# A two-layer encoder trunk on one Trainium2 core: P of two head groups turned by VectorE and DRAM, merged exits, new planner times

## The chip, the cores and the metric

The kernel runs on one core of a Trainium2 chip. The core has TensorE (matrix products; PE in the profile, with its weight loads as PEld), VectorE (DVE), ScalarE (ACT), GpSimd (POOL), SyncE (SP, which here only issues DMAs), and 16 DMA engines. TensorE writes into PSUM, eight banks of 512 f32 values in each of 128 partitions; the other engines read and write PSUM and the large on-chip memory SBUF. The metric is the device time of one execution in microseconds (us).

## The reference

Two layers work on x of 256 tokens by 1024 channels, all in f32:

```
x = x + 0.5 * swiglu(rmsnorm(x))                 # 1024 -> 2 x 2816 -> 1024
h = rmsnorm(x);  q_s, k_s, v_s, q_m = h @ w_in   # 1024 -> 768 + 768 + 768 + 256
layer 0: p = softmax(rmsnorm(q) k^T * scale + rel_bias), masked by chunks of 64 tokens   (12 heads of 64)
layer 1: p = softmax(q1 k1^T) - lam * softmax(q2 k2^T), with rotary and the block-causal mask (6 double heads)
o_s = p @ v;   o_m = 4-head attention into 256 memory tokens
x = x + concat(o_s, o_m) @ w_out
x = x + 0.5 * swiglu(rmsnorm(x))
```

swiglu(h) = (silu(h @ w_gate) * (h @ w_up)) @ w_down. The weights come from DRAM once, some 190 MB read in one execution.

## The kernel before

**Products.** Every f32 weight block is split into hi, rounded to the type fp32r, and lo = w - hi. `split_hi` (ScalarE, L378) and `split_lo` (VectorE, L398) do this for one item after another; an item is 128 x 2048 values, that is four blocks of 128 x 512. Activations are split in the same way (xh, xl). `dense` (L548) then issues three products of 128 x 128 by 128 x 512 on TensorE: xh·hi, xh·lo, xl·hi. Three raw buffers and four hi/lo buffers hold weights ahead of TensorE. Some product pairs in each SwiGLU go by a scheme with seven products in place of eight; the weight sums that it needs are the tiles `wsum` (L390), made by VectorE from pieces of 512 columns.

**Stages.** For each layer: SwiGLU 1 (`ffn`), mixer (`mixer`), SwiGLU 2. In a SwiGLU the 2816 hidden channels are 11 groups of 256. A group's gate and up lie side by side in one PSUM bank per token block of 128 (tile `gu`); two of the 11 groups are made from seven products (`pair_m`, `product`, `pair_sums`), whose sums end in SBUF. At its end a group leaves by `evac` (L732): ScalarE's silu, VectorE's multiplication by the row scale xr = 1/rms(x) and by silu, a VectorE transpose of 32 x 32 blocks into `hb`, a write to DRAM (`hd`) and a read back in another order (`hr`), which completes the transpose. Then comes the down projection, and `finish` adds half of it to x.

**The first mixer.** `proj` makes five projections of 48 products: q and k of head group 0, v, q and k of group 1, q and k of group 2, the rest of v with the memory q. A head group is four heads. `qk_evac` normalises q and k and turns them on TensorE; `scores` makes S; `attn_soft` (L1529) adds the bias and takes the softmax with VectorE and ScalarE; `p_transpose` (L1511) turns P by TensorE (tile `ptp`) and copies it to SBUF (`PT`); the products with v go to `AV` and leave as `oT`. For group c there are two units, token block 0 (128 keys) and 1 (256 keys). Group 3 is the memory attention. In the first mixer the bias table lies reversed in DRAM, and a 128 x 128 matrix with ones on the other diagonal, `flip`, turns q with its rows reversed, and P back. The output projection `outp` (L1744) takes groups 0 and 1 for both token blocks first, then 2 and 3.

**What sets the order.** The program is written out by a planner (`Flow`, L48). TensorE's dense products are in a fixed sequence; each advances a clock by `T_MM`, and whatever else has become ready by that clock, by fixed costs for each engine and a hand-over of `HOP`, is put into the instruction streams in between. DMAs get fixed delays. On the chip each engine takes its own instructions strictly in that order and waits for its operands. `loader` issues weight loads on SyncE's queue when a raw buffer is free; `FULL` is the planner's clock up to which other transfers are counted against the loads. Tiles come from counted pools (`Slots`): `banks` (8 PSUM banks), `g2` (19 SBUF tiles of 128 x 512), `g4` (12 of 128 x 1024). Where a count is exhausted the planner's thread waits; where `split_lo` waits, the lo parts of all later items wait behind it. `Gate` holds a unit's scores or AV back for up to some us, so that two units enter TensorE together.

Of the kernel before, what the change touches and what calls it, by code (L numbers as in the profile page):

```python
# [40 lines left out]
T_MM = 0.216  # L41
T_TR = 0.107
# [5 lines left out]
class Flow:  # L48
# [16 lines left out]
    def eng(self, e, dur):  # L65
        self.free[e] = max(self.free[e], self.now) + dur
        return self.free[e] + HOP
# [99 lines left out]

@with_exitstack
def kernel(
# [22 lines left out]
    pp = ctx.enter_context(tc.tile_pool(name="pp", bufs=8, space=PSUM))  # L192

    dram = ctx.enter_context(tc.tile_pool(name="dram", bufs=4, space=bass.MemoryType.DRAM))
    banks = Slots(flow, pp, "ps", 8)
# [8 lines left out]
    def bank(name, shape=(P, 4, P)):  # L204
        return banks.take(list(shape), F32, name)
# [6 lines left out]
    def load_x(tb, hf):  # L212
# [12 lines left out]
    flip = const.tile([P, P], F32, name="flip")  # L225
    nc.gpsimd.memset(flip, 0.0)
    nc.gpsimd.affine_select(out=flip, in_=flip, compare_op=ALU.not_equal, fill=1.0, base=-(P - 1),
                            pattern=[[1, P]], channel_multiplier=1)
# [16 lines left out]
    def gain_columns():  # L245
# [14 lines left out]
        banks.give()  # L260
# [12 lines left out]
    class Item:  # L273
# [3 lines left out]
        def __init__(self, raws, uses=8, w=1):  # L277
# [4 lines left out]
            self.sums, self.t = [], []  # L282
# [24 lines left out]
    FULL = 600.0  # L307
# [74 lines left out]
    def split_lo():  # L382
        for i, it in enumerate(items):
            if it.sums:
                yield lambda: all(r.raw is not None for r in it.raws) and g2.left >= it.takes + 2
                yield max(r.arrive for r in it.raws)
                it.t += [g2.take([P, 512], F32, "wsum") for _ in range(it.takes)]
                for j, (x, y) in enumerate(it.sums):
                    yield calm_v(i)
                    nc.vector.tensor_sub(it.t[j], x(), y())  # L390
                    it.st[j] = flow.dve(512)
# [10 lines left out]
            g2.give(it.gives)  # L402
# [36 lines left out]
    def pair_items(raws):  # L439
# [3 lines left out]
        def sums(need, x, y, held=None):  # L443
            it = Item(need, 4)
            it.t, it.takes = (held.t, 0) if held else ([], 4)
            at_ = lambda v, j: it.own(j, 1, v) if isinstance(v, int) else (lambda: v.t[j])
            it.sums = [(at_(x, j), at_(y, j)) for j in range(4)]
            it.units = [((lambda j=j: it.t[j]), j, 1, j) for j in range(4)]
            return it
# [14 lines left out]
        def m7():  # L464
            made["t3"] = sums([r22, r12], 0, 1)
            made["t3"].gives = 4
# [11 lines left out]
        def m4():  # L478
            made["t4"] = sums([r21], 0, made["t2"], made["t2"])
            made["t4"].gives = 4  # L480
# [109 lines left out]
    def turn(dst, src, flipped=False):  # L590
        nc.tensor.transpose(out=dst, in_=src, identity=flip if flipped else ident)  # L591
        return flow.pe(T_TR)

# [8 lines left out]
    class Xt:  # L602
        def __init__(self, keep=False):
# [3 lines left out]
            self.r = [sm.tile([P, 1], F32, tag="xr", name="xr", bufs=4) for _ in range(2)]  # L607
            self.t, self.th = ([[None] * KT for _ in range(2)] for _ in range(2))
# [6 lines left out]
    def prep_half(xt, tb, hf, gc, wait=0.0):  # L615
# [10 lines left out]
        banks.give()  # L626
# [60 lines left out]
    def prep_rstd(xt, tb):  # L687
# [4 lines left out]
        xt.rt[tb] = flow.now  # L692

# [7 lines left out]
    def finish(acc, tb, xt, gc, half, by_dram=False):  # L701
        for hf in range(2):
# [3 lines left out]
            if half:  # L706
                nc.vector.scalar_tensor_tensor(out=xs[tb][:, sl], in0=acc.ps[tb][hf], scalar=0.5, in1=xs[tb][:, sl],
# [3 lines left out]
            banks.give()  # L711
# [13 lines left out]
    def ffn(l, nm, xt, gc_next):  # L725
# [6 lines left out]
        def evac(g, ps, end, gives=None):  # L732


            hb = None
            for tb in range(2):
                yield lambda: end[tb] is not None and xt.rt[tb] is not None
                yield end[tb]
                yield g2.has(3)
                sil = g2.take([P, 256], F32, "sil")  # L740
                nc.scalar.activation(sil, ps[tb][:, 0:256], AF.Silu, scale=xt.r[tb])  # L741
                yield flow.act(256)
                h = g2.take([P, 256], F32, "h")
                nc.vector.scalar_tensor_tensor(out=h, in0=ps[tb][:, 256:512], scalar=xt.r[tb], in1=sil,  # L744
                                               op0=ALU.mult, op1=ALU.mult)
                t = flow.dve(256, 0.06)
                g2.give()
                (gives or (banks, banks))[tb].give()
                if hb is None:
                    hb = g2.take([P, 4, 2, 2, 32], F32, "hb")  # L750
                yield t
                nc.vector.transpose(out=hb[:, :, tb].rearrange("p b f j -> p f b j"),
                                    in_=h.rearrange("p (f b i) -> p f b i", f=2, b=4))
                t = flow.dve(256, 0.05)
# [65 lines left out]
        def seven_sums(ms, t):  # L820

            def into_x(tb, hf, v):
                sl = slice(hf * 512, (hf + 1) * 512)
                nc.vector.scalar_tensor_tensor(out=xs[tb][:, sl], in0=v, scalar=0.5, in1=xs[tb][:, sl],
# [12 lines left out]
            banks.give()  # L837
# [5 lines left out]
            banks.give()  # L843
# [5 lines left out]
            banks.give()  # L849
# [4 lines left out]
            banks.give()  # L854
# [5 lines left out]
        def plain_chunk(g, c, tbs, ks=range(4)):  # L860
            if g not in open_:
                flow.until(banks.has(2))
                open_[g] = [bank(f"gu{tb}", (P, 512)) for tb in range(2)], [None, None]
                flow.spawn(evac(g, *open_[g]))
            ps, end = open_[g]
            for tb in tbs:
                if len(tbs) == 1:
                    t = two_phases(ps[tb], xt, tb, plan[l, nm, "gu"][g, c], range(4 * c, 4 * c + 4), c == 0, c == 1)
# [3 lines left out]
                for k in ks:  # L872
                    kk = 4 * c + k
                    t = dense(ps[tb], xt.h[tb][:, kk, :], xt.l[tb][:, kk, :], lambda: xt.t[tb][kk],
# [32 lines left out]
        def pair_sums():  # L907
# [10 lines left out]
            banks.give()  # L918
# [5 lines left out]
            banks.give()  # L924
            plus(w, u2, pb["m5"])
            banks.give()
# [3 lines left out]
            banks.give()  # L930
            for m, (g, tb), x in (("m3", (1, 0), w), ("m2", (0, 0), u), ("m4", (0, 1), u2)):
# [3 lines left out]
                banks.give()  # L935
                pps[g][tb], pend[g][tb] = x, t

        def product(m):
# [5 lines left out]
            if m == "m1":  # L944
                flow.spawn(pair_sums())
                for e in range(2):
                    flow.spawn(evac(pair + e, pps[e], pend[e], (g2, g2)))
# [972 lines left out]
```

## Time and profile before

| | |
|---|---|
| Time, median of 3 runs | 946.02 us (945.81 to 946.78) |
| The profiled execution: time, span | 945.89 us, 944.1 us |
| Granted TensorE clock | 1.000 |
| Busy: TensorE, VectorE, ScalarE | 938.1, 830.6, 592.5 us |
| First mixer, first projection to last output product | 207.3 to 308.7 us of the span |
| Second mixer, the same | 662.1 to 765.5 us |
| DRAM read, written | 190.04 MB, 15.20 MB |

A row of instructions in order of time has start, duration, engine, line, operation, written tile <- read tiles, shape and count. A row of a group has line, engine, operation and tiles, then count, total busy time and mean nanoseconds of one, then idle time of the engine before them with what ended it. A row of DMA issues ends with the median time from issue to landing. A row by stretch of time has the length and then each engine's busy time with its number of instructions. TensorE's records overlap in its pipeline: a product is shown with 0.39 us while the next starts after less. L591 is the helper that issues every transpose on TensorE.

### The profile page before, as it was taken

To read this page: it belongs to the slowest core of one execution; us is meant where nothing else is said; L and a number is where in the kernel's file an instruction comes from. 1 tells how busy PE (TensorE), PEld (TensorE's weight loads), DVE (VectorE), ACT (ScalarE), POOL (GpSimd) and SP (SyncE) were. 2 spreads that over 40 slices of the span, in tenths; PEclk is the share of its full clock that TensorE was granted. 3 is DMA by queue.
4 is the path that set the end of the run, shared out by engine and by line. 5 is a ranking of instruction groups with operands and counts; after the bars stand their busy time and mean duration, and the time that the engine had idled before them with its cause. 6 is when DMAs were issued, how large, how long until landed. Compare 5 with 4: busy or idle time off the path is not lost. (4 is left out here: it accounts for less than half of the span.)

```text
span 944.1 us, 13356 instructions
## 1 busy us (share of the span) xinstructions
PE 938.1 (99%) x4469; PEld 772.6 (82%) x4469; DVE 830.6 (88%) x1506; ACT 592.5 (63%) x1129; POOL 107.2 (11%) x160
## 2 busy tenths in 40 slices
PE   9999999999999999999999999999999999999998
PEld 7888888888878888888888888888887788888886
DVE  6989888899886998988788998896989899998995
ACT  6656676677685756656555656664777765665671
POOL 0000028651210000000000000000334100000000
PEclk9999999999999999999999999999999999999999
DMA  9876899588425477887746588775632367689561
GB/s 299 261 245 197 262 365 336 203 275 275 148 91 178 133 237 228 258 292 239 242 157 219 192 257 262 256 249 169 223 120 70 126 222 223 198 269 315 182 217 47
DMA packets 172606, 206.13 MB, mean 218 GB/s; under 512 B 10297, under 2 KB 147322, under 8 KB 172538
## 3 DMA queue, kind: packets, MB, share of 16 engines
q1 hardware_dynamic: 169530, 202.92, 66.8%
q10 hardware_dynamic: 3008, 2.37, 0.8%
q8 instruction: 35, 0.57, 0.3%
q14 instruction: 33, 0.27, 0.1%
HBM read 190.04 MB, written 15.20 MB: 217 GB/s over the span
## 5 line engine op out<-in xcount | busy, mean ns | idle before, releaser
L398 DVE TENSOR_TENSOR lo<-raw,hi 128x512 fp32r<-128x512 f32 (+1 forms) x466 | 392.2, 876 | 38.5 <-ACT hi L378 37.8
L378 ACT CAST hi<-raw 128x512 fp32r<-128x512 f32 (+1 forms) x465 | 332.4, 769 | 141.2 <-DMA raw<-in_ffn_w_up_dram 34.7
L558 PE MATMUL gu<-lo,xh 128*128 128x512 f32 x528 | 205.7, 390 | 0.6 <-DVE lo L1816 0.6
L555 PE MATMUL gu<-hi,xh 128*128 128x512 f32 x528 | 205.8, 390 | 0.0
L561 PE MATMUL gu<-hi,xl 128*128 128x512 f32 x528 | 205.6, 389 | 0.0
L558 PEld LDWEIGHTS gu<-lo,xh 128*128 128x128 f32 x528 | 99.2, 188 | 21.5 <-DVE lo L1816 1.0
L561 PEld LDWEIGHTS gu<-hi,xl 128*128 128x128 f32 x528 | 99.1, 188 | 20.7
L555 PEld LDWEIGHTS gu<-hi,xh 128*128 128x128 f32 x528 | 99.3, 188 | 20.4
L561 PE MATMUL acc<-hi,ht 128*128 128x512 f32 x270 | 105.6, 391 | 0.0
L555 PE MATMUL acc<-hi,ht 128*128 128x512 f32 x270 | 105.1, 389 | 0.0
L558 PE MATMUL acc<-lo,ht 128*128 128x512 f32 x270 | 105.1, 389 | 0.0
L378 ACT CAST hi<-wsum 128x512 fp32r<-128x512 f32 x83 | 48.7, 618 | 26.8 <-DVE wsum L390 22.3
L558 PE MATMUL pj<-lo,xh 128*128 128x512 f32 x160 | 63.7, 398 | 0.0
L561 PE MATMUL pj<-hi,xl 128*128 128x512 f32 x160 | 63.6, 397 | 0.0
L555 PE MATMUL pj<-hi,xh 128*128 128x512 f32 x160 | 63.5, 397 | 0.0
L741 ACT ACTIVATE sil<-gu,xr 128x256 f32<-128x256 f32 x72 | 33.8, 471 | 42.9 <-PE gu L561 41.3
L558 PEld LDWEIGHTS acc<-lo,ht 128*128 128x128 f32 x270 | 50.7, 188 | 10.6
L561 PEld LDWEIGHTS acc<-hi,ht 128*128 128x128 f32 x270 | 50.7, 188 | 10.4
L555 PEld LDWEIGHTS acc<-hi,ht 128*128 128x128 f32 x270 | 50.7, 188 | 10.3
L598 POOL TENSOR_TENSOR xr<-v,nhalf 128x1 f32<-128x1 f32 x12 | 8.6, 720 | 435.0 <-DVE v L596 435.0
L398 DVE TENSOR_TENSOR lo<-wsum,hi 128x512 fp32r<-128x512 f32 x83 | 53.5, 681 | 0.0
L744 DVE SCALAR_TENSOR_TENSOR h<-gu,xr,sil 128x256 f32<-128x256 f32 x72 | 34.4, 478 | 7.2 <-ACT sil L741 6.7
(250 smaller groups left out, 1531.9 us busy)
## 6 DMA issues: line engine op xcount, KB each, us to landing
raw<-in_ffn_w_down_dram SPq DMA_DIRECT2D x176, 256.0 KB, 4.4
raw<-in_ffn_w_gate_dram SPq DMA_DIRECT2D x81, 512.0 KB, 4.2
raw<-in_ffn_w_up_dram SPq DMA_DIRECT2D x81, 512.0 KB, 5.4
raw<-in_w_in_dram SPq DMA_DIRECT2D x32, 512.0 KB, 5.4
hd<-hb SPq DMA_DIRECT2D x44, 256.0 KB, 4.8
hr<-hd SPq DMA_DIRECT2D x44, 256.0 KB, 4.7
raw<-in_w_out_dram SPq DMA_DIRECT2D x8, 1024.0 KB, 4.9
raw<-in_w_mem_kv_dram SPq DMA_DIRECT2D x4, 1024.0 KB, 6.1
```

The lines of the kernel that those rows point to most:

```text
L378: nc.scalar.copy(out=it.part(0, q, w), in_=src())
L398: nc.vector.tensor_sub(it.part(1, q, w), src(), it.part(0, q, w).bitcast(F32))
L555: nc.tensor.matmul(out=ps, lhsT=xh, rhs=wh, start=start, stop=False)
L558: nc.tensor.matmul(out=ps, lhsT=xh, rhs=wl, start=False, stop=False)
L561: nc.tensor.matmul(out=ps, lhsT=xl, rhs=wh, start=False, stop=stop)
L598: nc.gpsimd.tensor_tensor(out=dst, in0=v[:, :n], in1=nhalf[:, :n], op=ALU.pow)
L741: nc.scalar.activation(sil, ps[tb][:, 0:256], AF.Silu, scale=xt.r[tb])
L744: nc.vector.scalar_tensor_tensor(out=h, in0=ps[tb][:, 256:512], scalar=xt.r[tb], in1=sil, op0=ALU.mult, op1=ALU.mult)
```

## The change

Seven things are changed together.

1. **P of groups 0 and 1 in the first mixer** no longer goes through `p_transpose`. A thread `carried` per parity of heads calls `trip`: VectorE turns 32 x 32 blocks, ScalarE's queue writes the tile to DRAM and reads it back in the other order, and AV reads the tile that was read back. Group 2, the memory group and the second mixer stay as they were.
2. **No reversal.** The host lays the bias table out in full, one row per query position (128 x 12 x 256 values), `flip` is gone, and all turns use the identity.
3. **Merged exits.** PSUM is one tile of eight banks (`Banks`). A gate/up group takes two neighbouring banks, and one multiplication and one transpose of 512 columns serve both token blocks. The two banks come free together. The row scale leaves the multiplication: the down projection's result is multiplied by rh = xr / 2 when it is added to x.
4. **Wide pair sums.** The weight sums of the gate/up pairs are made in pieces of 1024 columns, in tiles of `g4` in place of `g2`.
5. **Shared exits of q and k** of the second token block: both ScalarE operations first, then both VectorE operations.
6. **Planner constants**: costs of products, transposes, scores and AV, the engines' hand-over, and `FULL`.
7. Two waits in the preparation of the memory tokens allow a slack of 0.4 us.

```
-T_MM = 0.216
-T_TR = 0.107
+T_S1, T_S3 = 0.0012, 0.0009
+T_AV1, T_AV2 = 0.127, 0.219
+HOP_E = 0.14
+T_MM = 0.2285
+T_TR = 0.09
...
     def eng(self, e, dur):
         self.free[e] = max(self.free[e], self.now) + dur
-        return self.free[e] + HOP
+        return self.free[e] + HOP_E
...
+class Banks:
...
+    def has_pair(self):
+        return lambda: any(b + 1 in self.free for b in self.free)
...
+    def take_pair(self):
+        age = self.free.index
+        b = min((b for b in self.free if b + 1 in self.free), key=lambda b: max(age(b), age(b + 1)))
+        return self._hold(self.tile[:, b:b + 2, :], (b, b + 1))
...
-    FULL = 600.0
+    FULL = 620.0
...
     def split_lo():
...
-                yield lambda: all(r.raw is not None for r in it.raws) and g2.left >= it.takes + 2
+                yield lambda: all(r.raw is not None for r in it.raws) and it.room.left >= it.takes + (2 if it.room is g2 else 0)
...
-            it.t, it.takes = (held.t, 0) if held else ([], 4)
+            it.t, it.takes = (held.t, 0) if held else ([], 2)
+            it.room = g4
...
+            it.sums = [(at_(x, j), at_(y, j)) for j in range(2)]
+            it.units = [((lambda j=j: it.t[j]), 2 * j, 2, j) for j in range(2)]
...
         xt.rt[tb] = flow.now
+        nc.gpsimd.tensor_scalar(out=xt.rh[tb], in0=xt.r[tb], scalar1=0.5, scalar2=None, op0=ALU.mult)
...
+                    nc.scalar.activation(sil[:, tb], ps[:, tb, 0:256], AF.Silu, scale=xt.r[tb])
+                    t = flow.act(256)
+                yield t
+                h = g2.take([P, 2, 2, 4, 32], F32, "h")
+                nc.vector.tensor_mul(h.rearrange("p t f b i -> p t (f b i)"), ps[:, :, 256:512], sil)
+                t = flow.dve(512, 0.06)
                 g2.give()
+                banks.give(ps)
+                hb = g2.take([P, 4, 2, 2, 32], F32, "hb")
                 yield t
+                nc.vector.transpose(out=hb.rearrange("p b t f j -> p (t f) b j"),
+                                    in_=h.rearrange("p t f b i -> p (t f) b i"))
...
             if g not in open_:
-                flow.until(banks.has(2))
-                open_[g] = [bank(f"gu{tb}", (P, 512)) for tb in range(2)], [None, None]
+                flow.until(banks.has_pair())
+                open_[g] = banks.take_pair(), [None, None]
...
+        def trip(src, n):
+            yield g2.has()
+            m = n // P
+            xb = g2.take([P, 4, m, 32], F32, "tb")
+            nc.vector.transpose(out=xb.rearrange("p b m j -> p m b j"), in_=src.rearrange("p (m i b) -> p m b i", b=4, i=32))
+            t = flow.dve(n, n / 1200.0)
+            g2.give()
+            yield t + 0.1
+            d = dram.tile([4, 32, 4, m * 32], F32, tag=f"td{m}", name="td", bufs=4)
+            nc.scalar.dma_start(out=d.rearrange("a i b x -> (a i) (b x)"), in_=xb.rearrange("p b m j -> p (b m j)"))
+            flow.act(0, 0.2)
+            carry(0.8)
+            yield flow.now + 4.5
+            g2.give()
+            yield g2.has()
+            r = g2.take([P, 4, m * 32], F32, "tr")
+            nc.scalar.dma_start(out=r, in_=d.rearrange("a i b x -> (i b) a x"))
+            flow.act(0, 0.2)
+            carry(0.8)
+            yield flow.now + 5.0
+            return r.rearrange("p a (m j) -> p m a j", j=32)
...
+        def carried(src, nk, pts, e):
+            r = yield from trip(src.rearrange("p a b -> p (a b)"), 2 * nk)
+            pts[e] = r.rearrange("p (a b) c j -> p a b c j", a=2)
...
             for e in range(2):
                 yield pes[e][6]
-                pt, t = yield from p_transpose(pes[e][0], nk, bias_t is not None)
-                pts.append(pt)
+                if grp < 2 and typ_a:
+                    flow.spawn(carried(pes[e][0], nk, pts, e))
+                    continue
+                pt, t = yield from p_transpose(pes[e][0], nk)
+                pts[e] = pt
+            yield lambda: None not in pts
             yield t
...
         if name == 'a_rel_bias':
-            a = _np.ascontiguousarray(_np.pad(a[0], ((0, 0), (0, 127)), mode='edge')[:, ::-1])
+            a = _np.pad(a[0], ((0, 0), (0, 127)), mode='edge')[:, ::-1]
+            a = _np.ascontiguousarray(_np.stack([a[:, 127 - p:383 - p] for p in range(128)]))
```

271 lines of the change are left out of this document (155 added, 116 removed).

## The prediction

> **What bounds the kernel now.** I read the busy shares of the page first, then the busy times by stage, then TensorE's instructions in order of time.
>
> ```profile
> PE 938.1 (99%) x4469; PEld 772.6 (82%) x4469; DVE 830.6 (88%) x1506; ACT 592.5 (63%) x1129; POOL 107.2 (11%) x160
> ...
> core 0: us, PE busy (x) PEld busy (x) DVE busy (x) ACT busy (x) POOL busy (x), PEclk, DMA share, GB/s
> 205.00:310.00 105.00, 105.00 (x634) 85.29 (x633) 86.06 (x232) 76.75 (x188) 15.95 (x10) 1.00 0.52 168
> 310.00:660.00 350.00, 350.00 (x1561) 289.79 (x1561) 310.80 (x502) 207.53 (x340) 2.88 (x4) 1.00 0.72 228
> 660.00:770.00 110.00, 109.54 (x608) 88.24 (x607) 100.62 (x214) 80.16 (x209) 32.47 (x29) 1.00 0.46 147
> ```
>
> TensorE sets the end. In the 350 us of the two middle SwiGLUs it has no idle time at all, at the full granted clock (1.00), while VectorE rests 39 us there. A busy TensorE hides short gaps, because its records overlap, so the steps from start to start count.
>
> ```profile
> 99.67 0.39 PE L561 MATMUL pair_m<-hi,xl 128*128 128x512 f32 x1
> ...
> 105.79 0.39 PE L561 MATMUL gu<-hi,xl 128*128 128x512 f32 x1
> ```
>
> Twenty-seven steps lie between these rows: 6.12 / 27 = 0.227 us for a dense product, with no gap. So work taken off VectorE or ScalarE in a SwiGLU is worth nothing. Time can come only from instructions that leave TensorE, and from waits inside the two mixers.
>
> **The transposes that go.** The first mixer turns P on TensorE; 36 of these are its three self-attention groups, 12 each (one per head pair, parity and key block: 4 for the first token block, 8 for the second). Two groups leave: 24. Their price is read around group 0, columns being start, duration, engine and line:
>
> ```profile
> 237.98 0.39 PE L558 MATMUL pj<-lo,xh 128*128 128x512 f32 x1
> 238.22 0.38 PE L591 MATMUL ptp<-flip,pe 128*128 128x128 f32 x2
> 238.35 0.48 PE L561 MATMUL pj<-hi,xl 128*128 128x512 f32 x1
> ...
> 240.50 0.60 PE L591 MATMUL ptp<-flip,pe 128*128 128x128 f32 x4
> 240.86 0.48 PE L558 MATMUL pj<-lo,xh 128*128 128x512 f32 x1
> ...
> 241.41 0.60 PE L591 MATMUL ptp<-flip,pe 128*128 128x128 f32 x4
> 241.76 0.48 PE L555 MATMUL pj<-hi,xh 128*128 128x512 f32 x1
> 242.08 0.39 PE L558 MATMUL pj<-lo,xh 128*128 128x512 f32 x1
> ```
>
> Between 237.98 and 242.08 twelve dense products start (those not shown stand under the dots), worth 12 x 0.227 = 2.72; the stretch takes 4.10. So 12 transposes cost 1.38 us: some 0.36 for four, and 0.09 because the dense product after each insertion takes 0.31 instead of 0.227. Two groups: **-2.8 us**, all of it on the engine that sets the end.
>
> **What P does instead.** Per group, token block and parity (8 trips): a VectorE block transpose, a write to DRAM and a read back, both issued on ScalarE's queue. The same route is in the trace for x:
>
> ```profile
> L636 DVE STREAM_TRANSPOSE xb<-x 128x512 f32<-128x512 f32 x4 | 4.4, 1094 | 0.0
> L1091 DVE STREAM_TRANSPOSE mb<-mem 128x256 f32<-128x256 f32 x8 | 4.7, 612 | 0.0
> L642 ACTq DMA_DIRECT2D xd<-xb x4: 326/332/336, 175.8 to 187.7; - x4
> L649 ACTq DMA_DIRECT2D xr<-xd x4: 376/378/379, 183.1 to 192.5; - x4
> xd<-xb ACTq DMA_DIRECT2D x4, 256.0 KB, 3.2
> xr<-xd ACTq DMA_DIRECT2D x4, 256.0 KB, 5.6
> DMA to landing us min/median/max: 2.4/5.0/6.2
> ```
>
> VectorE gains 4 x 1.094 + 4 x 0.612 = 6.8 us of work. ScalarE gains 16 issues, 8 x (0.332 + 0.378) = 5.7 us, and loses eight copies from PSUM. A trip after its transpose takes 0.33 + 3.2 + 0.38 + 5.6 = 9.5 us, and the planner's own figures for it, 4.5 + 5.0, add up to the same. Where a read lands 0.6 later (the longest of these eight took 6.2), TensorE waits at the AV products, which it meets in written order: 0 to 0.6 per group, I take 0.2: **+0.4 us**. On ScalarE the read's issue waits for the write, with exponentials and hi casts queued behind; the plan allows 4.5 for a write that took 3.2, so I cost that at nothing. AV now reads P in strips of 32 columns; no row shows TensorE doing so. Between no cost and a doubling of two groups' AV (about 1.5 us each, the row at 272.58 below) lies 0 to +3.0; I take 0, for the bytes per partition are the same.
>
> **Is P there in time?** Group 0's, turned by 241.8 in the rows above, is wanted only by the output projection. Group 1 is the test, for the output projection takes group 0, then group 1.
>
> ```profile
> 258.70 0.48 DVE L1170 SCALAR_TENSOR_TENSOR q<-qktp,gcs,q 128x256 fp32r<-128x256 f32 x1
> 260.06 0.71 PE L1506 MATMUL S<-qk 64*128 64x128 f32 x8
> 266.43 1.14 DVE L1571 TENSOR_SCALAR pe<-pe,rs 128x256 f32<-128x256 f32 x4
> 272.58 1.53 PE L1590 MATMUL AV<-PT,V 128*64 128x128 f32 x24
> 274.82 0.42 DVE L1598 TENSOR_TENSOR oT<-AV,oT 128x256 fp32r<-128x256 f32 x1
> 284.13 0.48 PE L555 MATMUL acc<-hi,oT 128*128 128x512 f32 x1
> ...
> 232.00:256.00 24.00, 24.00 (x147) 19.49 (x146) 18.59 (x58) 16.43 (x42) 5.66 (x3) 1.00 0.53 175
> 256.00:270.00 14.00, 14.00 (x91) 11.38 (x90) 12.34 (x49) 11.37 (x34) 2.65 (x2) 1.00 0.23 77
> ```
>
> P of group 1 is scaled at 267.6. With all four transposes behind it (2 x 0.612 + 2 x 1.094 = 3.4) the last block is ready at 271.0, back at 280.5, and through AV and its exit (from 272.58 to 274.82 + 0.42 in the rows, 2.7 us) at 283.2, on the old clock. The first product that needs it started at 284.13, and will be wanted 2.8 earlier, at 281.3. In its favour: group 0's transposes and AV (1.4 + 1.5) leave the stretch before S of group 1, so the chain can start 2.9 earlier: 280.3, one us to spare. Against it: VectorE was busy 30.9 of 38 us between 232 and 270 and gets 6.8 more, 37.7 of 38. lo splits yield to attention in the plan and run up to four weight buffers ahead, so I take no wait here, between a gain of nothing and a wait of 5.3 (the first rival).
>
> The Trainium skill speaks against the whole move: "VectorE: DVE Perf Modes", in "Rules for kernel authors", advises TensorE for a 128x128 transpose where PSUM will do as destination, since VectorE turns only 32x32 blocks. The trace agrees that the other route is longer, 9.5 us of trip against some 5 from scaled P to AV. By that rule the sum would be a loss, the size of the first rival; by the rows it is a gain as long as the trip is covered.
>
> **Parts that I cost at nothing**, because TensorE has no gap where they lie. Merged exits and wide pair sums:
>
> ```profile
> L752 DVE STREAM_TRANSPOSE hb<-h 128x256 f32<-128x256 f32 x88 | 38.4, 437 | 0.0
> L744 DVE SCALAR_TENSOR_TENSOR h<-gu,xr,sil 128x256 f32<-128x256 f32 x72 | 34.4, 478 | 7.2 <-ACT sil L741 6.7
> L741 ACT ACTIVATE sil<-gu,xr 128x256 f32<-128x256 f32 x72 | 33.8, 471 | 42.9 <-PE gu L561 41.3
> L390 DVE TENSOR_TENSOR wsum<-raw,wsum 128x512 f32<-128x512 f32 x52 | 34.2, 678 | 0.2
> L398 DVE TENSOR_TENSOR lo<-raw,hi 128x1024 fp32r<-128x1024 f32 x162 | 193.4, 1213 | 11.1 <-ACT hi L378 10.7
> ```
>
> Thirty-six exits fall from two multiplies and two transposes to one each (0.96 to about 0.68, the transposes alike): about 10 us of VectorE. Sixty-four sums of 0.68 become 32 of 1.21: 5 us. Both hide under dense products. What they cost if cover is gone: the two banks come free together, some 0.47 + 0.68 after the last product, and the hd write with the loads behind it on SP's queue about half a us later; weights are loaded several chunks ahead. The halved row scale is one small GpSimd operation per block; the reversal matrix is off every chain, q is turned by as many transposes as before; the bias load keeps its bytes. k and q of a second token block now share an exit (two ScalarE, then two VectorE operations), which if anything frees S earlier. All 0.
>
> **Order.** The planner's dense product goes from 0.216 to 0.2285 (measured: 0.227), its hand-over from 0.22 to 0.14. Planned cover for other engines' work therefore shrinks by 6% and 0.08 per hand-over. S of group 1 started at 260.06, 0.9 us after the last split of its q (258.70 + 0.48); a chain of 5 us with three or four hand-overs loses 0.3 + 0.3. That still covers. Waits do exist in the second mixer:
>
> ```profile
> 732.43 0.40 PE L555 MATMUL acc<-hi,oT 128*128 128x512 f32 x1
> 733.09 1.54 PE L1506 MATMUL S<-k,q 64*128 64x256 f32 x12 [0.26 <-ACT PT L1520]
> ...
> 736.26 0.39 PE L555 MATMUL acc<-hi,oT 128*128 128x512 f32 x1
> 736.71 0.44 PE L591 MATMUL otp<-ident,o 128*128 128x128 f32 x2
> ...
> 739.07 0.98 PE L1506 MATMUL S<-km,qmT 64*128 64x256 f32 x12
> ```
>
> Over the 0.227 of a step that is 0.43 before S and 0.22 before otp, and 0.56 within S (1.54 against 0.98 for the same block at 739.07): 1.2 us. The new times may remove these or make as many: -1.2 to +1.2, taken as 0, the constants pulling both ways.
>
> **Sum.** The profiled execution took 945.89 us (span 944.1 and 1.8 around it), 0.13 under the median of 946.02. 945.89 - 2.8 + 0.4 = 943.5; against the median **943.6 us**.
>
> **Rivals.**
> 1. *VectorE makes group 1 late.* If its queue does not let the chain start earlier, oT comes at 283.2 instead of 280.3, and if group 0's 3.4 us of transposes still stand in that queue, at 286.6: 5.3 after 281.3. TensorE, in order, waits with the rest of the output projection behind. 943.6 + 5.3 = 948.9. For it: 37.7 of 38 us; against it: VectorE idles 5.4 us between 232 and 256 with lo splits that can be put off. Slower than the median once oT passes 281.3 by 2.4.
> 2. *Small waits eat the gain.* Order +1.2 and 0.3 more at each of the two AVs: 943.6 + 1.8 = 945.4, no change. For it: thinner cover everywhere; against it: the first mixer had none of these waits before.
> 3. *No neighbouring banks.* An opening that finds no free pair waits for a closing exit, 0.47 x 2 + 0.68 and hand-overs, about 1.9. Three of these beside the pair products, which hold single banks: 943.6 + 5.7 = 949.3. Against it: eight banks, four or fewer in use at most openings.
>
> **Chances.** Forecast 0.56 (own range 941.3 to 944.9), first rival 0.15, second 0.20, third 0.09. Below 0.2% (1.9 us) a measurement of this kernel cannot tell a difference: faster means under 944.1, slower over 947.9. The forecast gives faster 0.52 and no change 0.04; the second rival 0.20 no change; the other two slower 0.13 + 0.07 and no change 0.04. So 0.52, 0.28, 0.20. The range goes from 940.8 (order -1.2, no wait at AV, and 1.2 for gaps in the second mixer too short to be seen singly) to 949.3.
>
> **What would show it.** No P transposes of groups 0 and 1 on TensorE, the first mixer's matmuls 24 fewer; the dense step still 0.227; the first product of group 1 in the output projection following its predecessor without a gap. A gap there proves the first rival, gaps before AV and S the second, gaps before the first product of a gate/up group the third. The forecast is wrong if the stretch of the first mixer is not 1.5 to 3 us shorter, or if any SwiGLU changes by over 0.5.

## The result, and the profile after

The changed kernel took **952.02 us** (median of 6 runs, 951.32 to 952.73); the kernel before, beside it on the same chip, 946.06 (945.81 to 946.78). The ratio is 1.0061, with a 95% interval of 1.0048 to 1.0074: slower by 6 us, where 943.6 was forecast and 949.3 was the end of the range.

The busy shares and the clock by slices, from the page of the changed kernel:

```profile
PE 939.5 (99%) x4445; PEld 771.2 (81%) x4445; DVE 820.6 (86%) x1378; ACT 582.2 (61%) x1087; POOL 110.1 (12%) x170
...
PEclk9999999989999999999999999999999999999999
```

The 24 matmuls are gone from TensorE (4469 to 4445), VectorE has 10 us less to do, where some 8 were worked out, and ScalarE 10 us less. The profiled execution took 952.73. One digit of the clock has fallen, in the ninth slice (190 to 214 us).

The busy times by stage of the changed kernel, for the same stretches and with the same columns as in the prediction:

```profile
205.00:310.00 105.00, 103.45 (x605) 82.81 (x605) 96.40 (x241) 76.28 (x187) 19.02 (x14) 1.00 0.71 228
310.00:660.00 350.00, 350.00 (x1561) 289.75 (x1560) 304.62 (x432) 206.21 (x323) 3.98 (x8) 1.00 0.69 226
660.00:770.00 110.00, 109.12 (x609) 87.99 (x609) 97.78 (x212) 76.00 (x202) 32.21 (x30) 1.00 0.44 144
```

The middle SwiGLUs are as they were: 1561 TensorE instructions in 350 us, no idle time. To find the loss I took the start of the first dense product of every stage. That of the first mixer, in TensorE's instructions of the kernel before:

```profile
207.34 0.39 PE L555 MATMUL pj<-hi,xh 128*128 128x512 f32 x1
```

and of the changed kernel:

```profile
216.37 0.39 PE L596 MATMUL banks<-hi,xh 128*128 128x512 f32 x1
```

The stage ahead of it, the projections of the memory tokens to keys and values, starts at 185.58 before and 185.65 after. It lasts 207.34 - 185.58 = 21.76 before and 30.72 after. The table has this for all the kernels run, in us, with the median of the timed runs, their number, and the ratio to the kernel before on the same chip. The stages are those of the one profiled execution of each kernel, whose time can lie up to 1.9 us from the median. The three SwiGLU stretches are left out; in all kernels they lie within 179.3 to 180.3, 353.33 to 353.38 and 172.96 to 172.99.

| kernel | median (n) | ratio, 95% | memory projections | first mixer | second mixer |
|---|---|---|---|---|---|
| before | 946.06 (6) | | 21.76 | 101.36 | 103.45 |
| changed | 952.02 (6) | 1.0061, 1.0048-1.0074 | **30.72** | 99.66 | 103.18 |
| hop_pool | 950.97 (4) | 1.0052, 1.0036-1.0069 | 21.76 | 100.81 | 109.21 |
| before_hop_pool | 951.30 (4) | 1.0052, 1.0037-1.0067 | 25.62 | 102.05 | 103.68 |
| sin_later | 948.25 (10) | 1.0019, 1.0010-1.0029 | 27.79 | 99.22 | 103.21 |
| sin_half | 949.21 (6) | 1.0034, 1.0023-1.0046 | 27.79 | 98.78 | 103.20 |
| sin_later_sp_read | 943.35 (8) | 0.9971, 0.9961-0.9981 | 21.79 | 99.67 | 103.17 |
| **chain_cost** | **943.16** (6) | **0.9970, 0.9959-0.9982** | 21.76 | 99.20 | 103.18 |
| chain_031 | 953.04 (4) | 1.0073, 1.0056-1.0090 | 26.95 | 101.93 | 103.22 |
| before_trips | 944.80 (10) | 0.9988, 0.9978-0.9997 | 21.76 | 100.03 | 103.46 |
| chain_cost_no_trips | 945.40 (10) | 0.9997, 0.9988-1.0006 | 23.23 | 101.26 | 103.22 |
| before_consts_chain | 947.92 (10) | 1.0020, 1.0011-1.0030 | 21.76 | 100.90 | 105.97 |
| chain_cost_m2 | 948.44 (10) | 1.0021, 1.0010-1.0032 | 22.75 | 99.20 | 105.79 |
| chain_cost_split_exits | 945.00 (10) | 0.9987, 0.9977-0.9996 | 22.73 | 100.25 | 103.17 |

So the changed kernel **loses 8.96 us in one stage of 22 us that the prediction does not mention**, and gains 1.70 in the first mixer, 0.27 in the second and 0.15 in sum elsewhere: 8.96 - 2.12 = 6.84, which is 952.73 - 945.89.

**What happens in that stage.** The waits of the changed kernel between 165 and 215 us (engine, operation and line, what it waited for, then us in total, times, longest):

```profile
ACT ropew L1367 <- POOL ropew L1336: 10.1, 1, 10.1
DVE ropeC L1377 <- ACT ropew L1368: 8.1, 1, 8.1
...
PE banks L596 <- ACT hi L417: 2.8, 1, 2.8
...
PE banks L599 <- DVE lo L438: 1.9, 4, 0.8
```

Line 1367 is the first of two sines that ScalarE computes for the rotary tables of the second layer, from angles that GpSimd reduces in a long chain of small operations. Nothing in the first layer needs them. ScalarE's instructions in order of time in the changed kernel:

```profile
167.91 1.31 ACT L1212 ACTIVATE memh<-mr,gcol 128x256 fp32r<-128x256 f32 x3
179.34 0.26 ACT L1367 ACTIVATE ropew<-ropew 128x64 f32<-128x64 f32 x1 [10.12 <-POOL ropew L1336]
...
182.40 0.49 ACT L1212 ACTIVATE memh<-mr,gcol 128x256 fp32r<-128x256 f32 x1
```

and the same view of the kernel before:

```profile
203.25 0.46 ACT L1185 ACTIVATE vm<-kv,mr 128x256 f32<-128x256 f32 x1
...
205.39 0.26 ACT L1298 ACTIVATE ropew<-ropew 128x64 f32<-128x64 f32 x1
```

Before, the sine stood at 205.39, behind the evictions of the memory projections, and waited for nothing. After, it stands ahead of the last `memh`, which those projections read. ScalarE reached it at 169.2 and stood still for 10.12 us; the splits of the weights (`hi`) and of the memory tokens queued behind it. TensorE's instructions in order of time show where that arrives:

```profile
188.79 0.40 PE L602 MATMUL banks<-hi,meml 128*128 128x512 f32 x1
191.99 0.79 PE L596 MATMUL banks<-hi,memh 128*128 128x512 f32 x1 [2.81 <-ACT hi L417]
193.56 0.79 PE L599 MATMUL banks<-lo,memh 128*128 128x512 f32 x1 [0.77 <-DVE lo L438]
194.15 0.63 PE L602 MATMUL banks<-hi,meml 128*128 128x512 f32 x1
...
197.56 0.58 PE L599 MATMUL banks<-lo,memh 128*128 128x512 f32 x1
197.98 0.39 PE L602 MATMUL banks<-hi,meml 128*128 128x512 f32 x1
```

From 188.79 to 197.98 there are 12 steps, worth 2.72 us at 0.227; they took 9.19. That is 6.47 of the 8.96; most of the rest is one wait before 188 and three after 207, 1.9 together. Of the 6.47, the steps of 3.20 and 1.57 across the two waits shown make up 4.3. The others are the clock's: the eight steps from 194.15 to 197.56 took 3.41 us, 0.426 each instead of 0.227. The busy times by stretch of the changed kernel:

```profile
170.00:180.00 10.00, 10.00 (x46) 8.28 (x45) 2.87 (x8) 0.26 (x1) 8.27 (x22) 1.00 0.39 145
...
190.00:200.00 10.00, 7.24 (x20) 5.42 (x21) 9.06 (x22) 5.87 (x14) 0.83 (x2) 0.66 0.94 312
193.00:198.00 5.00, 4.44 (x11) 3.48 (x12) 4.77 (x9) 2.19 (x6) 0.00 (x0) 0.50 0.92 319
```

and of the kernel before:

```profile
170.00:180.00 10.00, 10.00 (x46) 8.29 (x45) 7.90 (x16) 4.82 (x12) 5.41 (x12) 1.00 0.73 252
...
190.00:200.00 10.00, 10.00 (x46) 8.29 (x45) 9.90 (x21) 6.28 (x13) 8.38 (x15) 1.00 1.08 336
```

Between 170 and 180 TensorE is as busy as ever, on weights split earlier, but ScalarE works for 0.26 us and VectorE for 2.87 of 10. The store of split weights runs dry, and TensorE pays from 189 on. The granted clock is 0.50 from 193 to 198 and 0.66 over 190 to 200: (1 - 0.66) x 10 x 2 = 6.8 us at half clock.

**Why the sine moved.** Two groups of GpSimd's operations on that tile, in the kernel before (count, then min/median/max ns, first and last start):

```profile
L1267 POOL TENSOR_TENSOR ropew<-ropew x20: 318/434/682, 140.0 to 202.6; 128x64 f32<-128x64 f32 x20
...
L1277 POOL TENSOR_SCALAR ropew<-ropew x10: 371/402/719, 137.1 to 193.3; 128x64 f32<-128x64 f32 x10
```

and in the changed kernel:

```profile
L1336 POOL TENSOR_TENSOR ropew<-ropew x20: 318/326/655, 133.0 to 180.4; 128x64 f32<-128x64 f32 x20
...
L1346 POOL TENSOR_SCALAR ropew<-ropew x10: 370/378/722, 129.9 to 175.4; 128x64 f32<-128x64 f32 x10
```

The chain has 90 such operations. The planner books 0.25 us for each, adds the hand-over, and looks again only after a dense product. Before: 0.25 + 0.22 = 0.47, more than two products of 0.216, so three, 0.65. After: 0.25 + 0.14 = 0.39, less than two products of 0.2285, so two, 0.46. The 89 steps shrink from a planned 58 us to 41. On the chip they took 180.4 - 129.9 = 50.5. The planner put the sine 10 us too early, and 10.1 us is what ScalarE waited.

### The profile page after: what moved, and what is told of

Same layout as the page of the kernel before. It is cut to its first block, busy times and chain, and to the rows that moved or that the text cites. A ratio compares the mean times of both kernels' runs of the same rounds, so it can differ in the third digit from the quotient of the medians.

```text
span 950.8 us, 13163 instructions
## 1 busy us (share of the span) xinstructions
PE 939.5 (99%) x4445; PEld 771.2 (81%) x4445; DVE 820.6 (86%) x1378; ACT 582.2 (61%) x1087; POOL 110.1 (12%) x170
## 4 chain that ended last, share of the span: by engine, by line
PE 76%; DVE 10%; DMA 5%; POOL 5%; issue 2%; ACT 1%; SPq 1%; ACTq 0%; DVEq 0%
PE banks L596 22%; PE banks L602 22%; PE banks L599 22%; DVE lo L438 4%; PE banks L632 2%; PE banks L619 2%; DMA raw<-in_ffn_w_up_dram 2%; POOL ropew L1334 1%; PE banks L1604 1%; PE banks L625 1%; PE banks L1696 1%; POOL ropew L1336 1%; DMA xr<-xd 1%; ACT hi L417 1%; SPq L368 1%
## 5 line engine op out<-in xcount | busy, mean ns | idle before, releaser
L596 PE MATMUL banks<-hi,xh 128*128 128x512 f32 x736 | 288.8, 392 | 0.0
L599 PE MATMUL banks<-lo,xh 128*128 128x512 f32 x736 | 288.0, 391 | 0.5 <-DVE lo L1921 0.5
L602 PE MATMUL banks<-hi,xl 128*128 128x512 f32 x736 | 287.3, 390 | 0.0
L599 PEld LDWEIGHTS banks<-lo,xh 128*128 128x128 f32 x736 | 138.4, 188 | 29.1 <-DVE lo L1921 1.0
L596 PEld LDWEIGHTS banks<-hi,xh 128*128 128x128 f32 x736 | 138.3, 188 | 28.6
L602 PEld LDWEIGHTS banks<-hi,xl 128*128 128x128 f32 x736 | 138.3, 188 | 28.5
L596 PE MATMUL banks<-hi,ht 128*128 128x512 f32 x270 | 105.4, 390 | 0.0
L599 PE MATMUL banks<-lo,ht 128*128 128x512 f32 x270 | 105.3, 390 | 0.0
L602 PE MATMUL banks<-hi,ht 128*128 128x512 f32 x270 | 105.2, 390 | 0.0
L596 PEld LDWEIGHTS banks<-hi,ht 128*128 128x128 f32 x270 | 50.7, 188 | 10.5
L602 PEld LDWEIGHTS banks<-hi,ht 128*128 128x128 f32 x270 | 50.7, 188 | 10.4
L599 PEld LDWEIGHTS banks<-lo,ht 128*128 128x128 f32 x270 | 50.7, 188 | 10.4
```

Of the source, the lines that this page charges most:

```text
L596: nc.tensor.matmul(out=ps, lhsT=xh, rhs=wh, start=start, stop=False)
L599: nc.tensor.matmul(out=ps, lhsT=xh, rhs=wl, start=False, stop=False)
L602: nc.tensor.matmul(out=ps, lhsT=xl, rhs=wh, start=False, stop=stop)
```

## The experiments

**1. The hand-over of GpSimd alone.** In the changed kernel only GpSimd gets the old hand-over back; in the kernel before only GpSimd gets the new one.

```
# hop_pool, from the changed kernel
-        return self.eng("G", dur)
+        return self.eng("G", dur) + HOP - HOP_E
# before_hop_pool, from the kernel before
-        return self.eng("G", dur)
+        return self.eng("G", dur) - 0.08
```

> The changed kernel with one planner number put back: GpSimd's hand-over is 0.22 again, so that the chain of some 100 small GpSimd operations for the rotary tables is again spread over the order as before. Theory (the sine stands too early in ScalarE's order and blocks it for 10.1 us): no wait at the sine, the memory projections back from 30.7 to about 21.8 us, no half clock, time 943 to 944.5. Rival (VectorE or the trips through DRAM cost the time): 950 or more.

> The kernel before with that one number alone: GpSimd's hand-over 0.14 in place of 0.22, nothing else of the change. Theory of the early sine: ScalarE blocked by 5 to 10 us at the sine, the memory projections longer by 3 to 9 us, time 949 to 955. If the loss needs the trips, the merged exits or the new banks: 946, as before.

The second is the cleaner. With 0.08 us less in one number, the kernel before took 951.30, and its waits show the same one:

```profile
ACT ropew L1298 <- POOL ropew L1267: 7.3, 1, 7.3
```

Its memory projections grew by 3.86 us, with 3.4 us of half clock. In the first, the memory projections are back at 21.76, which takes back the whole 8.96; but at 950.97, far from the 943 to 944.5 expected, it is hardly better in sum, because the hand-over also serves GpSimd's operations in the second mixer, and there a new loss of 6.0 us arises, of which TensorE's instructions show one wait:

```profile
737.68 1.39 PE L1604 MATMUL banks<-km,qmT 64*128 64x256 f32 x9 [1.42 <-ACT pe L1728]
```

S of the memory group waits for a PSUM bank that ScalarE's exponentials still read. From 738.01 on, the granted clock there is 0.50 for 3.41 us. The cause is confirmed in its place, but this was not a remedy: one constant moves work in two stages.

**2. The price of the chain alone.** Only in the set-up of the rotary tables, GpSimd's operations are booked at 0.33, so that 0.33 + 0.14 = 0.47 is three products again; then at 0.31, where 0.45 is still under the two products' 0.457.

```
-            yield flow.pool(0.25)
+            yield flow.pool(0.33)      # chain_cost; 0.31 in chain_031; 12 places in rope_setup
```

> The changed kernel with the planner's cost of one operation of the rotary chain 0.33 in place of 0.25, and nothing else: the chain alone is spread as before, all other GpSimd operations keep the new hand-over of 0.14. If the whole loss is the early sine, and what is left of it with the hand-over put back came from the second mixer's GpSimd operations: memory projections 21.8 us, first mixer (projections and output) 98.5 to 99.5 against 101.4 before, second 103 to 104 against 103.5: 943 to 944.5. If the second mixer's waits are the price of any shift in the order: 947 or more.

> As chain_cost, but 0.31 in place of 0.33. The planner resumes the chain only after a dense product (0.2285): 0.31 + 0.14 = 0.45 is two products, 0.33 + 0.14 = 0.47 is three. If this step makes the loss: sines early again, ScalarE blocked by 5 to 10 us, 949 to 953, for 0.02 us in a constant. If the loss grows smoothly with the constant: 943 to 944.

With 0.33 the sine stands at 193.45 and waits for nothing, as ScalarE's instructions show:

```profile
193.45 0.26 ACT L1367 ACTIVATE ropew<-ropew 128x64 f32<-128x64 f32 x1
```

The busy times of chain_cost over the ten microseconds in which the changed kernel was at half clock:

```profile
190.00:200.00 10.00, 10.00 (x46) 8.29 (x45) 9.23 (x22) 9.69 (x20) 3.75 (x5) 1.00 1.01 334
```

TensorE has no idle time, at full clock, and the memory projections take 21.76 again. The time is **943.16 us, faster than both kernels** (0.9970, 0.9959 to 0.9982). With 0.31 the kernel took 953.04, and among its waits that of the sine is back:

```profile
ACT ropew L1367 <- POOL ropew L1336: 6.0, 1, 6.0
```

Two hundredths of a microsecond in a planned price make 10 us in the kernel, as much as the whole step from 0.33 to 0.25 (952.02). It is a threshold in the planner's order, not a cost that grows. Of the 8.0 us between the profiled executions (951.12 and 943.15) 5.19 lie in the memory projections; 2.73 more lie in the first mixer, where TensorE's waits of 0.46 and 0.58 us explain a part.

**3. The sines later, all else as changed.** A delay in the plan ahead of the two sines, 14 us or 5; then, with 14, the read-back of x issued on SyncE's queue instead of ScalarE's.

```
+        yield flow.now + 14.0           # 5.0 in sin_half
         nc.scalar.activation(sn, acc, AF.Sin, scale=S2PI)
...
-        nc.scalar.dma_start(out=r, in_=d.rearrange("a i b x -> (i b) a x"))   # sin_later_sp_read also
+        nc.sync.dma_start(out=r, in_=d.rearrange("a i b x -> (i b) a x"))
```

> The changed kernel with the two sines alone put 14 us of the planner's clock later; the GpSimd chain stays as dense as in the changed kernel. Early sine: no wait at it, 943 to 944.5. Rival (the dense GpSimd chain itself slows VectorE or ScalarE): still 950 or more.

> The same with the sines only 5 us later. Early sine: ScalarE blocked by about 5 us in place of 10, TensorE's pause in the memory projections under 2 us and so, if the half clock is the price of a pause, no half clock: 944 to 948. If the half clock has another cause than the pause, it stays and the time is over 948.

> As sin_later, with the read-back of x through DRAM issued on SyncE's queue in place of ScalarE's. If ScalarE's stand of 6.3 us at that read's issue, behind a slow write, made the loss that sin_later still had: memory projections from 27.8 down to 21.8 to 24, 942.5 to 946. If ropeC on VectorE, waiting for the sines, made it: still 27 or more, 948.

Moving the sines away took back only 2.93 of the 8.96 (3.77 in the medians), where nearly all of it was expected. ScalarE's instructions in sin_later show a second stand:

```profile
181.04 0.33 ACTq L684 DMA_DIRECT2D xd<-xb  x1
...
186.62 0.38 ACTq L691 DMA_DIRECT2D xr<-xd  x1
187.03 1.28 ACT L1368 ACT_TABLE_LOAD   x1 [6.34 <-DMA xd<-xb]
```

The read of x must wait for its write to land; the wait stands in ScalarE's stream, and what follows waits too, 6.34 us. In this run the two writes whose landing is recorded landed 2.1 and 7.3 us after issue. With 5 us, both waits are there, 4.50 at the sine and 6.25 behind the write. TensorE's pause was 2.1 us, not under 2, and 949.21 is over the forecast, so this run does not tell whether the half clock has another cause than the pause. With the read on SyncE's queue the memory projections took 21.79 and the kernel 943.35.

That the stand behind the write made the whole loss of sin_later is not shown, though, for ScalarE stands at the same read in chain_cost, as its instructions show:

```profile
184.23 0.38 ACTq L691 DMA_DIRECT2D xr<-xd  x1
184.70 0.62 ACT L417 CAST hi<-raw 128x512 fp32r<-128x512 f32 x1 [5.54 <-PE banks L602]
```

The write was issued at 177.01, and the read, which must wait for its landing, went out at 184.23, 7.2 us later, though the row names TensorE as what ended the wait. TensorE lost nothing there. chain_cost_no_trips and chain_cost_m2 (experiments 4 and 6) have the same instructions in the same order as chain_cost on every engine up to 235 us. Their stands took 6.54 and 6.44 us and ended at 187.12 and 186.15, and their memory projections are longer by 1.47 and 0.99 us. In sin_later the sines stand right behind the read, and VectorE waits for them for 5.1 us; with SyncE's queue that wait was gone too. So the order has two weak places, the sine behind GpSimd and the read-back behind a write that lands late. The second cost from nothing to 1.5 us where casts stand behind it; how the 6.03 us of sin_later divide between it and the sines isn't known.

**4. The route of P alone.** Trips and no reversal in the kernel before, with the old planner numbers and all other parts as before; and chain_cost with P of all groups turned by TensorE again.

```
# before_trips: adds trip, carried, the full bias table, and drops flip
+                if grp < 2 and typ_a:
+                    flow.spawn(carried(pes[e][0], nk, pts, e))
+                    continue
# chain_cost_no_trips: takes the three lines out
```

> The kernel before with the trips through DRAM for P of groups 0 and 1 and the table without reversal, planner numbers, exits and pair sums as before. The prediction's term: first mixer shorter by 2.4 to 2.8, all else as before, 943.3 to 944. If the trips are late for the output projection (first rival): a gap before group 1's first output product and 946 to 949.

> The kernel chain_cost with P of all groups turned by TensorE again. If the trips are worth 2.4 to 2.8: slower than chain_cost by that, first mixer near 101.4. If they are worth nothing: the same as chain_cost.

In the first mixer the trips are worth 101.26 - 99.20 = **2.06 us** from the second pair, and 1.33 in the kernel before, where a new wait between P transposes of other groups takes some of it (TensorE's instructions of before_trips):

```profile
283.87 0.70 PE L591 MATMUL ptp<-ident,pe 128*128 128x128 f32 x4 [0.65 <-DVE pe L1597]
```

As a whole, before_trips is faster by 0.12% (0.9988, 0.9978 to 0.9997), too little to rest on alone; 944.80 is short of the 943.3 to 944 expected. chain_cost_no_trips is 2.24 us slower than chain_cost in the medians, close to the 2.06, and no different from the kernel before: without the trips no gain is left that can be told from the noise. Its profiled execution, 946.67, was 1.27 above its median, and the 1.47 more in its memory projections come ahead of any trip.

**5. The new planner numbers alone.** The kernel before with all the new numbers, and the chain at 0.33.

> The kernel before with all new planner numbers of the change and the rotary chain's cost at 0.33: no trips, no merged exits. Prediction's term for the order: -1.2 to +1.2 against 946, the second mixer 102.3 to 104.7 against 103.5, the first 100.5 to 102.5. Rival (thin cover shows as waits in both mixers): 948 or more.

It took 947.92 (1.0020, 1.0011 to 1.0030), over the forecast and just under the rival's 948. The first mixer gained 0.46, the second lost 2.52. Its waits there:

```profile
PE qktp L594 <- DVE m L1413: 0.8, 2, 0.5
PE S L1509 <- ACT pe L1625: 0.6, 1, 0.6
```

The new numbers are no gain by themselves. In the changed kernel's structure they do no harm in the second mixer (103.18); why the old structure suffers was not pursued.

**6. A try for the second mixer.** In chain_cost, one more GpSimd price, that of an operation ahead of the q/k turns, from 2.1 to 2.8.

```
-                    yield flow.pool(2.1)
+                    yield flow.pool(2.8)
```

> As chain_cost, with the planner's cost of the second mixer's GpSimd rotary product 2.8 in place of 2.1. If TensorE's waits of 0.60, 0.42 and 0.24 before the q and k transposes there come from cover that is too thin for this operation: they go, 942 to 942.6. If VectorE or ScalarE is what is late there: 943, as chain_cost.

A miss. The waits before the q/k turns stayed, and the wait of S for a bank, seen in hop_pool, appeared:

```profile
735.63 0.97 PE L1604 MATMUL banks<-km,qmT 64*128 64x256 f32 x9 [1.70 <-ACT pe L1728]
```

(TensorE's instructions again.) The second mixer took 105.79 instead of 103.18, and the kernel 948.44 (945.70 to 950.51; 946.66 in the profiled execution).

**7. The exits one per token block.** In chain_cost, silu, multiplication and transpose again for each token block of 256 columns, in the two neighbouring banks.

```
-                nc.vector.tensor_mul(h.rearrange("p t f b i -> p t (f b i)"), ps[:, :, 256:512], sil)
+                    nc.vector.tensor_mul(h, ps[:, tb, 256:512], sil)
```

> As chain_cost, with the gate/up exits one per token block again (two multiplications, two transposes), still in neighbouring banks that come free together. The prediction put the merged exits at nothing: 943.2 within 0.5, each SwiGLU as in chain_cost within 0.1. If VectorE's saving of some 10 us in the SwiGLUs matters: slower by over 1.

The stretches with the later SwiGLUs are the same to 0.03 us (353.36 and 172.97); the first one is 0.78 longer, 0.4 of it a wait for x from DRAM. By its time the run meets the mark that was set for the rival: 945.00 is 1.84 us over chain_cost (2.36 in the profiled executions). By stage, the rest of the loss lies in the memory projections (0.97, where chain_cost_m2 lost 0.99 with chain_cost's own order) and the first mixer (1.05), whose longest wait is one before q/k turns:

```profile
223.26 0.44 PE L632 MATMUL banks<-ident,qkn 128*128 128x128 f32 x2 [0.82 <-DVE qkn L1127]
```

So merging the exits is worth nothing in the later SwiGLUs, where VectorE does less for it. Whether the first mixer's 1.05 us come from the order, which other bookings in a SwiGLU shift, or from this one execution, isn't shown.

## Why the prediction was wrong

**The step that failed is "Order"**, "taken as 0, the constants pulling both ways", with bounds of -1.2 to +1.2. The true term is about +9, in a stage that I had not looked at. Two things were wrong in it. I argued from averages (cover shrinks by 6% and by 0.08 for a hand-over), while the planner works in whole dense products: 0.08 less in a hand-over made three products into two for each of 89 steps in a row, 17 us. And I looked for its effect only where attention is, though the hand-over is in every engine's cost. The rows to work it out lay open: GpSimd's chain before ran from 137.1 to 202.6, 0.74 us a step where the planner had booked 0.65, so a new booking of 0.46 was far below the pace that the trace had shown. The sine had to move ahead of its operand, and ScalarE would stand. I named what queues behind a wait for the trips only, not for the instructions that the new numbers would move.

**The sum without that step.** In chain_cost, where the sine stands right and all other parts are as changed, the time is 943.16; the forecast was 943.6. Its terms:

- *Transposes, -2.8.* They left, and the dense step stayed at 0.227. With the trips' own costs in it, the first mixer is 2.06 us shorter; I had -2.8 + 0.4 = -2.4. The mechanism was right, the size 0.3 too large, as far as single executions tell (99.20 in chain_cost, 99.66 in the changed kernel). Whether fewer changeovers go than I counted (0.09 at each of six) or the AV insertions cost more, the runs don't tell apart.
- *The trip, 9.5 us.* VectorE's block transposes took what x's had taken (1087 ns against 1094), the four writes whose landing is recorded took 1.7 to 2.5 us where I had 3.2, and the four such reads a median of 4.8 where I had 5.6. *AV from strips costs 0*: right, 281 ns against 277 for the same instruction. The groups of the changed kernel:

```profile
L1580 DVE STREAM_TRANSPOSE tb<-pe 128x512 f32<-128x512 f32 x4 | 4.3, 1087 | 0.0
...
L1696 PE MATMUL banks<-tr,V 128*64 128x128 f32 x48 | 3.5, 281 | 0.0
```

and of the kernel before:

```profile
L1590 PE MATMUL AV<-PT,V 128*64 128x128 f32 x72 | 4.8, 277 | 0.0
```

- *Is P there in time?* Yes, and the chain came out as worked out up to P's return. This stage starts 9.03 us later than before (216.37 against 207.34); the times "on the old clock" are less that. Group 1's last block transposes ended at 277.07, 268.0 on the old clock, and its last reads, issued at 282.71 and 283.27, landed in 3.0 and 3.2 us, by 277.5 on the old clock. With the 2.9 in its favour I had 268.1 and 277.6. So VectorE did not make group 1 late, and the first rival's cause is false. What I had wrong is the step from there to `oT`. TensorE's rows around the output projection, in the changed kernel:

```profile
281.00 0.39 PE L596 MATMUL banks<-hi,oT 128*128 128x512 f32 x1
...
290.41 0.39 PE L596 MATMUL banks<-hi,oT 128*128 128x512 f32 x1
...
291.54 0.39 PE L602 MATMUL banks<-hi,oT 128*128 128x512 f32 x1
291.77 1.91 PE L632 MATMUL banks<-ident,pe 128*128 128x128 f32 x16
293.61 1.09 PE L1696 MATMUL banks<-tr,V 128*64 128x128 f32 x16
294.53 1.04 PE L1696 MATMUL banks<-PT,vm 128*64 128x128 f32 x16
...
296.38 1.02 PE L1604 MATMUL banks<-km,qmT 64*128 64x256 f32 x12
297.33 0.50 PE L596 MATMUL banks<-hi,oT 128*128 128x512 f32 x1
```

Group 1's first product is the 25th of the output projection, at 290.41, so at 281.4 on the old clock; I had said wanted at 281.3. But the AV of its second token block stands in the order only at 293.61, 7.1 us after its P was back, and its `oT` after that: some 7 us later than the 280.3 I worked out, later even than the rival's 286.6. That price the rival had wrong too: between the 30th product at 291.54 and the 31st at 297.33 TensorE did the P transposes, AVs and S of the other units, 5.8 us of work that had to be done anyway, without a gap. I had treated the wait for P as idle time; the planner's dense sequence waits, TensorE doesn't.
- *Merged exits, wide sums, neighbouring banks: 0.* Right. VectorE's work in the middle SwiGLUs fell from 310.8 to 304.6 us, and the stretch is 353.37 against 353.36. The third rival is false.
- *Waits in the second mixer, 1.2 at most to gain.* 0.27 was gained. The second rival has support only in chain_cost's relatives (before_consts_chain, chain_cost_m2), not in the changed kernel.

Of the two tests that I set, "1.5 to 3 us shorter" in the first mixer (1.70) and no SwiGLU changed by over 0.5, both were met, and the kernel was slower all the same: they covered the stages that I had costed, and a test of the whole must cover the others.

The rule that I cited against the move, from the Trainium skill, "VectorE: DVE Perf Modes", section "Rules for kernel authors" (TensorE for 128x128 transposes), is not borne out here: with the trip covered, leaving TensorE was worth 2.06 us, since TensorE sets the end.

**What stays open.** The slack in the memory preparation, the wide pair sums and the shared q/k exits were not tried one by one; with chain_cost at 943.16 their sum with the rest is no loss. What a late write of x costs, and so how far the memory projections vary from execution to execution, was seen only in single profiles. Why the old structure loses 2.5 us in the second mixer under the new numbers wasn't settled.

## What to carry to other kernels

Where a planner writes the order, a changed price is a change of the program: before trusting it, list the long chains that it books (how many steps, what the trace says of one, what the new number says) and ask for each instruction that consumes such a chain what stands behind it on its engine. An instruction that nobody needs soon, placed 10 us early on an engine that executes in order, can cost more than all the work that a change saves; here booking the chain at three products a step (0.69 us, where its steps then took 0.64) in place of two turned a loss of 6 us into a gain of 3. Set the tests of a forecast so that they cover every stage, the untouched ones too.

## What the runs showed of the hardware

**Half clock after short pauses.** In the changed kernel, before_hop_pool, sin_half and sin_later the granted clock fell to half after TensorE had paused in the memory projections. The busy times of the changed kernel in two stretches of 3.41 us, one behind the other, with the columns of the prediction (the granted clock is 1.00, then 0.50):

```profile
187.72:191.13 3.41, 1.43 (x5) 0.86 (x5) 3.38 (x14) 0.72 (x2) 0.04 (x1) 1.00 0.66 220
191.14:194.55 3.41, 1.79 (x3) 1.11 (x4) 3.41 (x7) 2.90 (x7) 0.78 (x2) 0.50 0.91 303
```

and of one in chain_031, which paused too and kept the full clock:

```profile
201.24:204.65 3.41, 1.81 (x8) 1.22 (x7) 3.41 (x8) 2.92 (x6) 0.67 (x2) 1.00 0.86 271
```

The stretches are the clock's own steps: the trace of the changed kernel has 184.32 us at full clock, 6.83 at half and 754.35 at full, which are 54, 2 and 221 times 3.413, and in every kernel run the clock changed only after a whole number of them. In the memory projections the loss follows a step in which TensorE was busy for only 1.33 to 1.53 us (1.33 in sin_half, 1.43 in the changed kernel, 1.45 in before_hop_pool, 1.53 in sin_later), whether it idled in one pause (2.1 us in sin_half) or in several (at most 1.4 in sin_later). The full clock outlasted steps with 1.81 in chain_031 and 1.61 near the end of before_trips. But hop_pool lost it in the second mixer after a step with 1.99, so busy time as the profile shows it is not the whole rule. In the changed kernel half clock makes up about 2 of the 8.96 us. The Trainium skill, "TensorE: Matmul & The Clock Gate", section "What's actually happening", has two clock states and a window of about 3.4 us of idleness to lose the full clock, as many of work to regain it. The lengths at half clock here are one and two such windows; but no pause before the loss was that long (2.8 us the longest), so here the rows decide.

**A DRAM write under the weight stream** landed in 2.1 to 7.3 us in one and the same kernel (x in sin_later), and ScalarE, which issues the read-back, stood until it had landed: 5.54 us in chain_cost, 6.34 in sin_later, 6.54 in chain_cost_no_trips.
